# Attention scores by groups of four heads in TensorE's rows, and moved earlier in a two-layer hybrid encoder

## The chip, the cores and the metric

The kernel runs on one core of a Trainium2 chip. The metric is the device time of one execution in microseconds (us), the median of several executions.

## The reference

An encoder of two layers over 256 tokens with 1024 channels, in float32. Each layer mixes tokens in three parallel branches (multi-head latent attention, a convolution module, bidirectional retention), merges them by gates, and applies a SwiGLU block. The change concerns the attention branch alone:

```python
def mla_branch(c_q, c_kv, k_pe, cos, sin, q_norm, w_uq, kv_norm, w_ukv, w_o):
    q = (rms_norm(c_q, q_norm) @ w_uq).reshape(B, S, MLA_HEADS, MLA_NOPE + MLA_ROPE)   # 8 heads, 64 + 32
    q_nope = q[..., :MLA_NOPE]
    q_pe = apply_rope(q[..., MLA_NOPE:], cos, sin)
    kv = (rms_norm(c_kv, kv_norm) @ w_ukv).reshape(B, S, MLA_HEADS, MLA_NOPE + MLA_V)  # 8 heads, 64 + 64
    k_nope, v = kv[..., :MLA_NOPE], kv[..., MLA_NOPE:]
    k_pe = apply_rope(k_pe, cos, sin)                                                  # one key for all heads
    scale = (MLA_NOPE + MLA_ROPE) ** -0.5
    ...
        s = (jnp.einsum('bqhd,bkhd->bhqk', qn, k_nope)
             + jnp.einsum('bqhr,bkr->bhqk', qp, k_pe))
        p = jax.nn.softmax(s.astype(jnp.float32) * scale, axis=-1).astype(v.dtype)
        return jnp.einsum('bhqk,bkhd->bqhd', p, v)
    ...
    return o @ w_o
```

A head's score is the sum of a plain part over 64 channels and a rotary part over 32 channels, whose key all heads share.

## The kernel before

Activations lie transposed (channels on the 128 partitions, the 256 tokens along the row) as two halves in fp32r, `hT`; every weight is loaded in units of 128x1024, of which ScalarE makes the high half (`whi`, a cast, L175) and VectorE the low half (`wlo`, a subtraction, L177). Each product is three fp32r matmuls (L186, L187, L188). There are 9 buffers for high halves and 8 for low halves, so a unit is made some 8 units before TensorE reads it.

A layer runs, in TensorE's order: the latent projections, four groups for the convolution module, the up-projections of the attention (`up_T`, L577), then four groups for the retention's queries and keys (RQ, RQ, RK, RK: `feat_group`, 48 matmuls of 256 columns each, in two halves of 24), then three groups of its values and gates (RV, RG, RG: `tok_group`, four units of 12 matmuls of 512 columns each), then the gate groups and everything behind.

Small work of other branches is put between these matmuls. The list `pe_steps` holds closures; `feat_group` takes one from it after each of its halves, `tok_group` one after each of its units. So the place of a step in the list decides after which half or unit TensorE meets it. The steps of attention are:

- `qpe_T` (L602): transposes of the rotated query parts, copied to `qT`.
- `mla_b(pr)` (L626): the scores of a pair of heads, four fp32 matmuls over 96 rows, into two PSUM banks from the pool `tp` of four; then VectorE's row maximum `nm` (L629), ScalarE's exponentials into `pe` with sums `sme` (L634), VectorE's reciprocal (L636) and ScalarE's scaling of `pe` (L639).
- `mla_c(pr)` (L651): eight transposes of `pe`, copied by ScalarE to `pT` (L652).
- `mla_d(pr)` (L662): the products with the values `vtok`, two heads side by side in 64 columns each, split to `oTr`.

The four pairs' b, c and d steps (12) fill the 12 places of the RV, RG and RG groups: b(0) after RV's first unit, b(1) after the second, c(0) after the third, and so on to d(3) after the last unit of the second RG group.

VectorE also does the convolution: 124 operations per layer on `cacc` (L531, L534; "taps" below), which wait in a list of their own, `vec_steps`, two of which are issued with each weight unit. A list scheduler orders the instructions of every engine when the program is built, by its own estimate of when each can start; at run time each engine works through its own list in that order.

The score rows of a head lie in one buffer, plain part on partitions 0 to 63 and rotary part on 64 to 95, which is why each up-projection bank (two heads above each other on 128 partitions) is copied out in two activations of 64 partitions (L577), and the rotary parts in four of 32 (L605).

Of the kernel before, what the change touches and what calls it, by code (L numbers as in the profile page):

```python
# [58 lines left out]
def tile_hybrid_encoder(  # L59
# [63 lines left out]
    warm = act.tile([P, 512], BF16, tag="half", name="warm", bufs=7)  # L123
# [205 lines left out]
    kpad = cst.tile([P, NB, QK], F32, tag="kpad", name="kpad")  # L329
    G.memset(kpad, 0.0)  # L330

    def setup_tables():
# [3 lines left out]
        pos_r = act.tile([P, 512], I32, tag="half", name="pos_r", bufs=7)[:, :SEQ]  # L336
# [72 lines left out]
    for l in range(DEPTH):  # L409
# [23 lines left out]
        kT = big("kT").rearrange("p (h n) -> p h n", h=MH)  # L433
# [19 lines left out]
        def latent(pa, b):  # L453
# [11 lines left out]
            tk = sm.tile([P, ROPE], F32, tag="tk", name="tk", bufs=2)  # L465
            rope(kpad[:, b, NOPE:].rearrange(V4, h=1, j=2),
                 pa[:, QR + KVR:C_CONV].rearrange(V4, h=1, j=2),
                 cosr[:, b, :], sinr[:, b, :], tk.rearrange(V4, h=1, j=2))

            def f():  # L470
                pc = tp()
                for j in range(3):
                    T.transpose(pc[:, j * P:(j + 1) * P], cn[:, j * P:(j + 1) * P], ident)
                T.transpose(pc[:QK, 3 * P:4 * P], kpad[:, b, :], ident)
# [68 lines left out]
        qT = big("qT").rearrange("p (h n) -> p h n", h=MH)  # L543
# [45 lines left out]
        for c in range(2):  # L589
            up_T(qT[:, 4 * c:4 * c + 4, :], un[c], 0, (cTh, cTl), 0, 2, sc)()  # L590
        for c in range(2):
            up_T(kT[:, 4 * c:4 * c + 4, :], uk, c, (cTh, cTl), 2, 1, 1.0)()
# [5 lines left out]
        def qpe_T():  # L598
# [10 lines left out]
        for g in range(2):  # L609
            feat_group(win, C_RQ + g * 256, hT, KT, ret_rope(rqT, g))  # L610
        for g in range(2):
            feat_group(win, C_RK + g * 256, hT, KT, ret_rope(rkT, g))
# [5 lines left out]
        NPR = MH // 2  # L618
        pTs, pes = {}, {}

        def mla_b(pr):
            def f():
                for b in range(NB):
                    ps = tp()
                    for j in range(2):
                        T.matmul(ps[:, j * SEQ:(j + 1) * SEQ], qT[:QK, 2 * pr + j, b * P:(b + 1) * P],  # L626
                                 kT[:QK, 2 * pr + j, :], start=True, stop=True)
# [4 lines left out]
                    for j in range(2):  # L632
                        js = slice(j * SEQ, (j + 1) * SEQ)
                        S.activation(pe[:, js], ps[:, js], AF.Exp, bias=nm[:, j:j + 1],  # L634
                                     accum_out=sme[:, j:j + 1])
                    V.reciprocal(sme, sme)  # L636
                    for j in range(2):
                        js = slice(j * SEQ, (j + 1) * SEQ)
                        S.activation(pe[:, js], pe[:, js], AF.Copy, scale=sme[:, j:j + 1])  # L639
                    pes[pr, b] = pe  # L640
            return f

        def mla_c(pr):
            def f():
                pT = mid("pT").rearrange("p (h k n) -> p h k n", h=2, k=2)
                pTs[pr] = pT
                for b in range(NB):
                    pe = pes.pop((pr, b))
                    pt = tp()
                    for jk in range(4):  # L650
                        T.transpose(pt[:, jk * P:(jk + 1) * P], pe[:, jk * P:(jk + 1) * P], ident)  # L651
                    S.copy(pT[:, :, :, b * P:(b + 1) * P],  # L652
                           pt.rearrange("p (h k n) -> p h k n", h=2, k=2))
# [29 lines left out]
        def ret_a(h):  # L683
            def f():
# [17 lines left out]
                sh = act.tile([P, 512], F32R, tag="half", name="sTh", bufs=7)  # L702
                sl = act.tile([P, 512], F32R, tag="half", name="sTl", bufs=7)
# [284 lines left out]
```

## Time and profile before

| | |
|---|---|
| median of 3 runs | 934.07 us (933.36 to 934.19) |
| profiled execution: its own time | 933.89 us |
| profiled execution: span of the trace | 932.1 us |
| granted TensorE clock, mean | 0.998 |
| TensorE matmul busy | 924.0 us (99% of the span) |
| VectorE busy | 689.0 us (74%) |
| ScalarE busy | 530.9 us (57%) |

Busy time of TensorE counts from a matmul's start to its modelled end, and neighbours overlap; what a matmul costs is read from the distance of its start to the next one's. Times in the trace count from the start of the span, which is 1.8 us shorter than the execution's own time.

### The profile page before, as it was taken

The page shows a single profiled execution, that of the slowest core. Times are in us where ns is not written, and L with a number is a line of the kernel's source. Part 1 is how long each engine was busy: PE and PEld are TensorE (multiplying, and loading weights), DVE is VectorE, ACT ScalarE, POOL GpSimd, SP SyncE. Part 2 cuts the span into 40 slices and gives each one's busy share as a digit, 9 for nine tenths or more (in the row PEclk, how much of TensorE's full clock was granted, in tenths as well). Part 3 has the DMA queues.
Part 4 walks back from the last instruction along what each step waited for, and adds up shares of the span by engine and source line. Part 5 has one row for each costly group of instructions (what it writes and reads, how often), then busy time and mean ns, then how long its engine had stood idle before and what let it go on. Part 6 is the DMA issues. An engine that isn't in the chain of part 4 may idle for free.

```text
span 932.1 us, 13255 instructions
## 1 busy us (share of the span) xinstructions
PE 924.0 (99%) x4924; PEld 788.9 (85%) x4924; DVE 689.0 (74%) x1101; ACT 530.9 (57%) x821; POOL 36.7 (4%) x77
## 2 busy tenths in 40 slices
PE   9999999999999999999999999999999999999997
PEld 6999878888888888888889997788888888888885
DVE  6789999996657766664485899999766676666532
ACT  5774786545545655554365758755454556566421
POOL 2000000000010000000120000010000100000000
PEclk9999999999999999999999999999999999999999
DMA  6885455565637766666377655545656376665621
GB/s 226 250 270 161 137 173 164 158 185 185 191 88 234 248 183 191 191 203 193 100 210 204 183 157 174 188 136 162 200 181 177 123 236 191 194 186 182 214 79 45
DMA packets 113214, 166.70 MB, mean 179 GB/s; under 512 B 5929, under 2 KB 62905, under 8 KB 113150
## 3 DMA queue, kind: packets, MB, share of 16 engines
q1 hardware_dynamic: 113150, 165.87, 58.5%
q8 instruction: 38, 0.62, 0.3%
q14 instruction: 26, 0.21, 0.1%
HBM read 164.80 MB, written 1.05 MB: 178 GB/s over the span
## 4 chain that ended last, share of the span: by engine, by line
PE 97%; DMA 1%; ACT 0%; DVE 0%; SPq 0%; issue 0%; DVEq 0%; POOLq 0%; POOL 0%; ACTq 0%
PE acc L186 20%; PE acc L187 19%; PE acc L188 19%; PE acc L251 12%; PE acc L253 7%; PE acc L205 6%; PE acc L208 3%; PE acc L254 2%; PE tp L626 1%; PE tp L662 1%; PE tp L651 1%; DMA raw<-in_w_in_dram 1%; PE tp L692 1%; PE tp L283 1%; PE tp L187 1%; PE tp L188 1%
## 5 line engine op out<-in xcount | busy, mean ns | idle before, releaser
L177 DVE TENSOR_TENSOR wlo<-raw,whi 128x1024 fp32r<-128x1024 f32 (+1 forms) x300 | 362.7, 1216 | 119.7 <-PE acc L187 58.4
L175 ACT CAST whi<-raw 128x1024 fp32r<-128x1024 f32 (+1 forms) x300 | 312.2, 1048 | 200.9 <-PE acc L188 120.5
L251 PE MATMUL acc<-hT,whi 128*128 128x512 f32 x504 | 127.8, 393 | 0.0
L186 PE MATMUL acc<-whi,hT 128*128 128x512 f32 x288 | 118.2, 410 | 0.0
L187 PE MATMUL acc<-wlo,hT 128*128 128x512 f32 x288 | 112.7, 391 | 0.0
L188 PE MATMUL acc<-whi,hT 128*128 128x512 f32 x288 | 112.6, 391 | 0.0
L251 PEld LDWEIGHTS acc<-hT,whi 128*128 128x128 f32 x504 | 94.7, 189 | 18.3
L534 DVE SCALAR_TENSOR_TENSOR cacc<-apad,ccol,cacc 128x256 f32<-128x256 f32 x240 | 108.4, 479 | 1.3
L253 PEld LDWEIGHTS acc<-hT,wlo 128*128 128x128 f32 x576 | 78.6, 190 | 5.6
L253 PE MATMUL acc<-hT,wlo 128*128 128x256 f32 x576 | 80.3, 282 | 0.0
L186 PE MATMUL acc<-hT,whi 128*128 128x256 f32 x256 | 73.2, 286 | 0.0
L188 PE MATMUL acc<-hT,wlo 128*128 128x256 f32 x256 | 72.5, 283 | 0.0
L187 PE MATMUL acc<-hT,whi 128*128 128x256 f32 x256 | 72.5, 283 | 0.0
L186 PE MATMUL acc<-whi,hidh 128*128 128x512 f32 x176 | 68.6, 390 | 0.0
L188 PE MATMUL acc<-whi,hidl 128*128 128x512 f32 x176 | 68.5, 389 | 0.0
L187 PE MATMUL acc<-wlo,hidh 128*128 128x512 f32 x176 | 68.5, 389 | 0.0
L186 PEld LDWEIGHTS acc<-whi,hT 128*128 128x128 f32 x288 | 54.2, 188 | 13.3 <-issue 3.1
L188 PEld LDWEIGHTS acc<-whi,hT 128*128 128x128 f32 x288 | 54.1, 188 | 12.1
L187 PEld LDWEIGHTS acc<-wlo,hT 128*128 128x128 f32 x288 | 54.3, 189 | 10.1
L205 PE MATMUL acc<-whi,hT 128*128 128x512 f32 (+1 forms) x128 | 49.6, 389 | 0.4 <-ACT hT L182 0.3
L186 PEld LDWEIGHTS acc<-hT,whi 128*128 128x128 f32 x256 | 49.1, 192 | 0.2
L187 PEld LDWEIGHTS acc<-hT,whi 128*128 128x128 f32 x256 | 49.1, 192 | 0.2
(248 smaller groups left out, 1478.3 us busy)
## 6 DMA issues: line engine op xcount, KB each, us to landing
raw<-in_w_in_dram SPq DMA_DIRECT2D x112, 512.0 KB, 4.0
raw<-in_ffn_w_gate_dram SPq DMA_DIRECT2D x44, 512.0 KB, 4.3
raw<-in_ffn_w_up_dram SPq DMA_DIRECT2D x44, 512.0 KB, 4.6
raw<-in_ffn_w_down_dram SPq DMA_DIRECT2D x44, 512.0 KB, 4.4
raw<-in_ret_w_o_dram SPq DMA_DIRECT2D x16, 512.0 KB, 3.7
raw<-in_w_out_dram SPq DMA_DIRECT2D x16, 512.0 KB, 3.7
raw<-in_mla_w_o_dram SPq DMA_DIRECT2D x8, 512.0 KB, 4.4
raw<-in_conv_w_pw_dram SPq DMA_DIRECT2D x8, 512.0 KB, 3.7
```

Of the source, the lines that this page charges most:

```text
L175: S.copy(hi, raw)
L177: V.tensor_sub(lo, raw, hi.bitcast(F32))
L186: T.matmul(o, lh, rh, start=start, stop=False)
L187: T.matmul(o, lh, rl, start=False, stop=False)
L188: T.matmul(o, ll, rh, start=False, stop=stop)
L205: T.matmul(o, ah[:, 2 * i + k, :], w[:, k, :], start=not (i or k or n), stop=False)
L208: T.matmul(o, al[:, 2 * i - 2 + k, :], units[i - 1][0][:, k, :], start=False, stop=i == len(units) and k == 1)
L251: T.matmul(ps, units[k // 4][0][:, k % 4, js], both[:, k, :], start=k == 0, stop=False)
L253: T.matmul(ps[:, SEQ:], units[k // 4][1][:, k % 4, js], both[:, k, :SEQ], start=False, stop=False)
L254: T.matmul(ps, units[-1][0][:, 3, js], both[:, KT - 1, :], start=False, stop=True)
L283: T.transpose(ps[:, j * P:(j + 1) * P], hn[:, (4 * c + j) * P:(4 * c + j + 1) * P], ident)
L534: V.scalar_tensor_tensor(cacc[:, j, :], src, ccol[:, j, w:w + 1], cacc[:, j, :], op0=ALU.mult, op1=ALU.add)
```

## The change

The plain parts of two heads now lie above each other on the 128 partitions (`qn`, `kn`: four such pairs), and the rotary parts of four heads likewise (`qp`; the shared key `kp` is repeated four times). So an up-projection bank leaves in one activation of 128 partitions, and so do the rotary parts. A score is now the sum of two matmuls in a PSUM bank: one over 64 rows (two heads occupy the two halves of TensorE's rows) and one over 32 rows (four heads, four quarters). One `mla_b` step does four heads: 8 matmuls over 64 rows and 8 over 32, into all four `tp` banks, one for each head. There are two such steps instead of four, and c and d stay per pair. The steps start earlier: right after `qpe_T` in the RQ groups, not in RV.

```diff
-        return act.tile([P, 1024], F32, tag="mid", name=name, bufs=5)
+        return act.tile([P, 1024], F32, tag="mid", name=name, bufs=7)
...
-        return act.tile([P, 512], F32, tag="half", name=name, bufs=7)
+        return act.tile([P, 512], F32, tag="half", name=name, bufs=9)
...
-    kpad = cst.tile([P, NB, QK], F32, tag="kpad", name="kpad")
-    G.memset(kpad, 0.0)
+    kpad = cst.tile([P, NB, 4, ROPE], F32, tag="kpad", name="kpad")
...
-                S.copy(kT[NOPE:QK, :, b * P:(b + 1) * P],
-                       pc[NOPE:QK, 3 * P:4 * P].unsqueeze(1).broadcast_to([ROPE, MH, P]))
+                T.transpose(pc[:, 3 * P:4 * P], kpad[:, b].rearrange("p r n -> p (r n)"), ident)
+                S.copy(kp[:, b * P:(b + 1) * P], pc[:, 3 * P:4 * P])
...
-                pv = pq.rearrange("p (j n) -> p j n", j=2)
-                for i in range(2):
-                    S.activation(dst[:NOPE, i::2, :], pv[i * NOPE:(i + 1) * NOPE], AF.Copy, scale=scale)
+                S.activation(dst, pq.rearrange("p (j n) -> p j n", j=2), AF.Copy, scale=scale)
...
-            pv = pt.rearrange("p (g n) -> p g n", g=2)
-            for i in range(4):
-                S.copy(qT[NOPE:QK, i::4, :], pv[i * ROPE:(i + 1) * ROPE])
-        pe_steps.append(qpe_T)
+            S.copy(qp, pt.rearrange("p (g n) -> p g n", g=2))
...
-        def mla_b(pr):
+        def mla_b(qd):
+            def f():
+                banks = [tp() for _ in range(4)]
+                def out(r, b):
+                    return banks[r][:, b * SEQ:(b + 1) * SEQ]
+                for p in range(2):
+                    for b in range(NB):
+                        for i in range(2):
+                            hs = slice(i * NOPE, (i + 1) * NOPE)
+                            T.matmul(out(2 * p + i, b), qn[hs, 2 * qd + p, b * P:(b + 1) * P],
+                                     kn[hs, 2 * qd + p, :], start=b == 0, stop=False)
                 for b in range(NB):
-                    ps = tp()
-                    for j in range(2):
-                        T.matmul(ps[:, j * SEQ:(j + 1) * SEQ], qT[:QK, 2 * pr + j, b * P:(b + 1) * P],
-                                 kT[:QK, 2 * pr + j, :], start=True, stop=True)
+                    for r in range(4):
+                        rs = slice(r * ROPE, (r + 1) * ROPE)
+                        T.matmul(out(r, b), qp[rs, qd, b * P:(b + 1) * P], kp[rs, :], start=False, stop=b == 1)
+                for r in range(4):
+                    ps = banks[r]
...
-        for t in range(NPR + 2):
-            for d, stage in ((0, mla_b), (1, mla_c), (2, mla_d)):
-                if 0 <= t - d < NPR:
-                    pe_steps.append(stage(t - d))
+        pe_steps.extend([qpe_T, nop, mla_b(0), nop, nop, mla_c(0), mla_c(1), mla_d(0),
+                         mla_d(1), mla_b(1), nop, nop, mla_c(2), mla_c(3), mla_d(2), mla_d(3)])
+        for g in range(2):
+            feat_group(win, C_RQ + g * 256, hT, KT, ret_rope(rqT, g))
+        for g in range(2):
+            feat_group(win, C_RK + g * 256, hT, KT, ret_rope(rkT, g))
```

The small operations per bank (maximum, exponentials, reciprocal, scaling) are as many as before and of the same shapes; the four heads of a step come behind each other. The shared rotary key is made in as many VectorE operations as before.

Where the first scores stand in VectorE's list, before: the end of the second RK rotation (L446 to L450 is one rotation of a group's output), and then the maxima `nm` of the first pair, each with one tap (L534) between.

```order
L446 TENSOR_TENSOR rkT<-acc,cosT 128x512
L448 TENSOR_TENSOR rt<-acc,sinT 64x512
L449 TENSOR_TENSOR rt<-acc,sinT 64x512
L534 SCALAR_TENSOR_TENSOR cacc<-apad,ccol,cacc 128x256
L450 TENSOR_TENSOR rkT<-rkT,rt 128x512
L534 SCALAR_TENSOR_TENSOR cacc<-apad,ccol,cacc 128x256
L629 TENSOR_REDUCE nm<-tp 128x2
L534 SCALAR_TENSOR_TENSOR cacc<-apad,ccol,cacc 128x256
L629 TENSOR_REDUCE nm<-tp 128x2
```

The same place in the changed kernel, from the end of the first RQ rotation on (taps are L538, maxima L635, reciprocals L641 there):

```order
L449 TENSOR_TENSOR rt<-acc,sinT 64x512
L538 SCALAR_TENSOR_TENSOR cacc<-apad,ccol,cacc 128x256
L450 TENSOR_TENSOR rqT<-rqT,rt 128x512
L538 SCALAR_TENSOR_TENSOR cacc<-apad,ccol,cacc 128x256
L177 TENSOR_TENSOR wlo<-raw,whi 128x1024
L538 SCALAR_TENSOR_TENSOR cacc<-apad,ccol,cacc 128x256 x11
L635 TENSOR_REDUCE nm<-tp 128x2 x4
L538 SCALAR_TENSOR_TENSOR cacc<-apad,ccol,cacc 128x256
L177 TENSOR_TENSOR wlo<-raw,whi 128x1024
L641 RECIPROCAL sme<-sme 128x2 x2
L446 TENSOR_TENSOR rqT<-acc,cosT 128x512
```

Eleven taps stand ahead of the four maxima, and the rotation of the second RQ group, which stood five rows behind the first one's end, now stands behind the maxima and two reciprocals.

Where the second four heads' scores stand in VectorE's list of the changed kernel (before, the corresponding third pair's two maxima stood behind one `wlo` and the two halves of `vrl`):

```order
L177 TENSOR_TENSOR wlo<-raw,whi 128x1024
L538 SCALAR_TENSOR_TENSOR cacc<-apad,ccol,cacc 128x256 x8
L535 TENSOR_SCALAR cacc<-apad,ccol 128x256
L538 SCALAR_TENSOR_TENSOR cacc<-apad,ccol,cacc 128x256
L635 TENSOR_REDUCE nm<-tp 128x2 x3
L641 RECIPROCAL sme<-sme 128x2
L635 TENSOR_REDUCE nm<-tp 128x2
L641 RECIPROCAL sme<-sme 128x2
```

Ten taps stand ahead of these maxima. Between the two places VectorE's list of the changed kernel holds the rotations of the last three groups, six `wlo` units, the low halves of the first two `oTr` parts and single taps.

ScalarE's list for the second four heads in the changed kernel (exponentials are L640, scalings L644, `pT` copies L659):

```order
L640 ACTIVATE pe,sme<-tp,nm 128x256 x4
L644 ACTIVATE pe<-pe,sme 128x256 x4
L640 ACTIVATE pe,sme<-tp,nm 128x256 x4
L644 ACTIVATE pe<-pe,sme 128x256 x4
L182 CAST vrh<-acc 128x512 x2
L175 CAST whi<-raw 128x1024 x2
L659 COPY pT<-tp 128x512 x2
```

The scaling of the first of the four heads stands behind the exponentials of the first two; the copies of the first `pT` stand behind all four heads, two `vrh` and two weight casts.

## Rows read from the trace of the kernel before

**Rows 1.** The page: busy time of the engines, share of the span, instructions.

```profile
PE 924.0 (99%) x4924; PEld 788.9 (85%) x4924; DVE 689.0 (74%) x1101; ACT 530.9 (57%) x821; POOL 36.7 (4%) x77
```

**Rows 2.** Stretches: length, busy us (instructions) of PE, PEld, DVE, ACT, POOL, clock.

```profile
71.80:112.10 40.30, 40.30 (x255) 36.40 (x253) 40.06 (x71) 24.91 (x53) 0.00 (x0) 1.00 0.54 156
528.70:569.00 40.30, 40.30 (x254) 36.45 (x253) 40.06 (x71) 26.20 (x54) 0.00 (x0) 1.00 0.54 156
```

**Rows 3.** Timeline of TensorE: start, duration, line, rows*columns of the array, shape, count.

```profile
68.65 0.28 PE L187 MATMUL acc<-hT,whi 128*128 128x256 f32 x1
...
88.68 0.40 PE L186 MATMUL acc<-whi,hT 128*128 128x512 f32 x1
...
91.43 1.89 PE L626 MATMUL tp<-kT,qT 96*128 96x256 f32 x8
...
93.40 0.40 PE L187 MATMUL acc<-wlo,hT 128*128 128x512 f32 x1
```

**Rows 4.** Timeline of TensorE at mla_d(0), two heads in 64 columns each.

```profile
112.38 1.08 PE L662 MATMUL tp<-pT,vtok 128*64 128x256 f32 x8
...
113.73 0.40 PE L187 MATMUL acc<-wlo,hT 128*128 128x512 f32 x1
```

**Rows 5.** Timeline of TensorE where it goes to 34 and then 8 rows.

```profile
36.23 0.28 PE L188 MATMUL acc<-hT,wlo 128*128 128x256 f32 x1
36.44 0.43 PE L503 MATMUL tp<-ident,prow 34*128 34x34 f32 x4
36.80 0.23 PE L504 MATMUL tp<-ident,grow 8*128 8x8 f32 x1
```

**Rows 6.** Timeline of VectorE in layer 0: one rotation, and a run of the other operations.

```profile
72.78 0.69 DVE L446 TENSOR_TENSOR rqT<-acc,cosT 128x512 f32<-128x512 f32 x1
...
74.90 0.49 DVE L534 SCALAR_TENSOR_TENSOR cacc<-apad,ccol,cacc 128x256 f32<-128x256 f32 x1
75.31 0.69 DVE L450 TENSOR_TENSOR rqT<-rqT,rt 128x512 f32<-128x512 f32 x1
75.91 0.48 DVE L534 SCALAR_TENSOR_TENSOR cacc<-apad,ccol,cacc 128x256 f32<-128x256 f32 x1
...
103.69 2.05 DVE L534 SCALAR_TENSOR_TENSOR cacc<-apad,ccol,cacc 128x256 f32<-128x256 f32 x5
105.66 1.22 DVE L177 TENSOR_TENSOR wlo<-raw,whi 128x1024 fp32r<-128x1024 f32 x1
106.79 1.28 DVE L183 TENSOR_TENSOR vrl<-acc,vrh 128x512 fp32r<-128x512 f32 x2
107.99 1.28 DVE L629 TENSOR_REDUCE nm<-tp 128x2 f32<-128x512 f32 x2
109.19 0.87 DVE L534 SCALAR_TENSOR_TENSOR cacc<-apad,ccol,cacc 128x256 f32<-128x256 f32 x2
109.97 0.16 DVE L636 RECIPROCAL sme<-sme 128x2 f32<-128x2 f32 x1
110.05 0.86 DVE L534 SCALAR_TENSOR_TENSOR cacc<-apad,ccol,cacc 128x256 f32<-128x256 f32 x2
```

**Rows 7.** Timeline of TensorE at mla_c(0) and mla_c(1).

```profile
100.38 1.25 PE L651 MATMUL tp<-ident,pe 128*128 128x128 f32 x8
...
108.68 1.03 PE L651 MATMUL tp<-ident,pe 128*128 128x128 f32 x8
...
109.78 0.40 PE L187 MATMUL acc<-wlo,hT 128*128 128x512 f32 x1
```

**Rows 8.** Timeline of ScalarE behind the third pair's maxima.

```profile
108.72 0.50 ACT L634 ACTIVATE pe<-tp,nm 128x256 f32<-128x256 f32 x1
...
110.53 1.74 ACT L639 ACTIVATE pe<-pe,sme 128x256 f32<-128x256 f32 x4
112.13 2.02 ACT L175 CAST whi<-raw 128x1024 fp32r<-128x1024 f32 x2
114.02 1.10 ACT L652 COPY pT<-tp 128x512 f32<-128x512 f32 x2
```

More of the change, by code (lines that the diff above doesn't have):

```diff
@@ L122, in tile_hybrid_encoder @@
     V.memset(ones, 1.0)
-    warm = act.tile([P, 512], BF16, tag="half", name="warm", bufs=7)
+    warm = act.tile([P, 512], BF16, tag="half", name="warm", bufs=9)
     G.memset(warm, 0.0)
@@ L335, in setup_tables @@
                           allow_slow_non_contiguous=True)
-        pos_r = act.tile([P, 512], I32, tag="half", name="pos_r", bufs=7)[:, :SEQ]
+        pos_r = act.tile([P, 512], I32, tag="half", name="pos_r", bufs=9)[:, :SEQ]
         nc.sync.dma_start(pos_r, positions[0].partition_broadcast(P))
@@ L432, in tile_hybrid_encoder @@
         cTh, cTl = (cT[:, i * 768:(i + 1) * 768].rearrange("p (k n) -> p k n", k=3) for i in range(2))
-        kT = big("kT").rearrange("p (h n) -> p h n", h=MH)
+        kT = big("kT")
+        kn, kp = kT[:, :1024].rearrange("p (h n) -> p h n", h=MH // 2), kT[:, 1024:1024 + SEQ]
         vrh, vrl = (big(n, F32R).rearrange("p (b n) -> p b n", b=NB) for n in ("vrh", "vrl"))
@@ L464, in latent @@
                                    op0=ALU.mult, op1=ALU.mult)
[L465 to L468, printed above, removed]
+            tk = sm.tile([P, 2, 2, HR], F32, tag="tk", name="tk", bufs=2)
+            kr = pa[:, QR + KVR:C_CONV].rearrange("p (j n) -> p j n", j=2)
+            V.tensor_tensor(tk[:, 0], kr, cosr[:, b, :].unsqueeze(1).broadcast_to([P, 2, HR]), op=ALU.mult)
+            V.tensor_tensor(tk[:, 1, 0, :], kr[:, 1, :], sinr[:, b, :], op=ALU.mult)
+            V.tensor_tensor(tk[:, 1, 1, :], kr[:, 0, :], sinr[:, b, :], op=ALU.mult)
+            for j, op in enumerate((ALU.subtract, ALU.add)):
+                V.tensor_tensor(kpad[:, b, :, j * HR:(j + 1) * HR],
+                                tk[:, 0, j, :].unsqueeze(1).broadcast_to([P, 4, HR]),
+                                tk[:, 1, j, :].unsqueeze(1).broadcast_to([P, 4, HR]), op=op)
             def f():
@@ L540, in tile_hybrid_encoder @@
         drain(pe_steps)
-        qT = big("qT").rearrange("p (h n) -> p h n", h=MH)
+        qT = big("qT")
+        qn, qp = (qT[:, i:i + n * SEQ].rearrange("p (h n) -> p h n", h=n) for i, n in ((0, MH // 2), (1024, 2)))
         vtok = mid("vtok").rearrange("p (b h d) -> p b h d", b=NB, h=MH)
@@ L589, in tile_hybrid_encoder @@
         for c in range(2):
[L590 removed]
+            up_T(qn[:, 2 * c:2 * c + 2, :], un[c], 0, (cTh, cTl), 0, 2, sc)()
         for c in range(2):
[L592 removed]
+            up_T(kn[:, 2 * c:2 * c + 2, :], uk, c, (cTh, cTl), 2, 1, 1.0)()
         for b in range(NB):
@@ L631, in f @@
                     sme = sm.tile([P, 2], F32, tag="sme", name="sme")
[L632 to L635, printed above, removed]
+                    for b in range(NB):
+                        bs = slice(b * SEQ, (b + 1) * SEQ)
+                        S.activation(pe[:, bs], ps[:, bs], AF.Exp, bias=nm[:, b:b + 1], accum_out=sme[:, b:b + 1])
                     V.reciprocal(sme, sme)
[L637 to L640, printed above, removed]
+                    for b in range(NB):
+                        bs = slice(b * SEQ, (b + 1) * SEQ)
+                        S.activation(pe[:, bs], pe[:, bs], AF.Copy, scale=sme[:, b:b + 1])
+                    pes[4 * qd + r] = pe
             return f
@@ L646, in f @@
                 pTs[pr] = pT
-                for b in range(NB):
-                    pe = pes.pop((pr, b))
+                for j in range(2):
+                    pe = pes.pop(2 * pr + j)
                     pt = tp()
[L650 to L653, printed above, removed]
+                    for k in range(NB):
+                        for b in range(NB):
+                            T.transpose(pt[:, k * SEQ + b * P:k * SEQ + (b + 1) * P],
+                                        pe[:, b * SEQ + k * P:b * SEQ + (k + 1) * P], ident)
+                    S.copy(pT[:, j], pt.rearrange("p (k n) -> p k n", k=2))
             return f
@@ L701, in f @@
                                            op0=ALU.mult, op1=ALU.mult)
-                sh = act.tile([P, 512], F32R, tag="half", name="sTh", bufs=7)
-                sl = act.tile([P, 512], F32R, tag="half", name="sTl", bufs=7)
+                sh = act.tile([P, 512], F32R, tag="half", name="sTh", bufs=9)
+                sl = act.tile([P, 512], F32R, tag="half", name="sTl", bufs=9)
                 split(sh, sl, sT)
```

8 lines of the change are left out of this document (1 added, 7 removed).

## The prediction

> **What bounds the kernel now.** I read the page first: matmuls are busy 99% of the span [rows 1]. So the time is the sum of what TensorE works through, plus its waits. I then read the timeline of TensorE, start to start. A 512-column matmul takes 0.23 us (12 of them from 88.68 to 91.43), a 256-column one 0.12 us (167 from 68.65 to 88.68) [rows 3]. A pair's scores, four fp32 matmuls recorded as eight, push the next products back by 93.40 - 91.43 - 0.23 = 1.74 us, 0.435 us for one, and nothing more is lost at their edges [rows 3]. Any matmul time saved here comes straight off the total, unless TensorE has to wait instead.
>
> So the second reading is of who could make it wait. In the stretch where the attention steps will now lie, VectorE is busy 40.06 of 40.30 us, in both layers alike [rows 2]. It works through a fixed list without gaps, mostly taps that nobody needs soon, and it is not late for TensorE: only one c step waits, the first, whose eight records last 1.25 us where another's last 1.03, so 0.22 us [rows 7]. Idle time of VectorE could absorb a badly placed tap; there is none. This decides the case.
>
> **TensorE's own work.** Four heads cost 2 x 1.74 = 3.48 us before. Now there are eight matmuls over 64 rows and eight over 32. No row shows two matmuls in different rows at once. The nearest is mla_d, two heads in different columns: eight 256-column records take only about four slots, with 113.73 - 112.38 - 0.23 = 1.12 us behind their start [rows 4]. I take rows to overlap as columns do: four slots for the plain pairs, two for the rotary fours, six of 0.435 us, 2.61 us together. Edges: going from 128 rows to 34 costs 0.21 us in place of 0.12, so 0.09 [rows 5]; with that, mla_d costs 1.21 us, of which two slots are 0.87 and going in and out 0.34. The step to 32 rows between plain and rotary parts lies between 0.09 (the 34 to 8 rows' start, after four short transposes) and some 0.2 with a weight load laid bare; I take 0.2 [rows 4, 5]. A block is then 2.61 + 0.34 + 0.20 = 3.15 us. The gain is 0.33 us for four heads, **0.66 us per layer**. Ends: without any overlap the block is 16 x 0.435 + 0.54 = 7.5 us; with the pairs alone 12 x 0.435 + 0.54 = 5.8.
>
> The 0.22 us wait of the first c step goes too. The c and d steps stay at 109.78 - 108.68 - 0.23 = 0.87 us [rows 7] and 1.21. The fewer ScalarE copies (up-projections, rotary parts, shared key) save engine time that TensorE was not waiting for; I cost them at nothing. They are covered on both sides: an earlier copy meets the same matmul stream. The wider key operations are small, and the larger pools take no time.
>
> **What is late next.** TensorE ends the first RQ group at 88.68 - 144 x 0.12 = 71.4 us, as before. By the new order it meets, after RQ's second group's first half, the first score block, three halves later c(0), and so on. VectorE begins the first rotation when that bank is there: at the earliest 71.4, before at 72.78 [rows 6]; with ScalarE's copies out of the way I take 71.8. Durations, start to start [rows 6]: a rotation 2.12 + 0.60 = 2.72; a tap 1.97/5 = 0.394; a `wlo` 1.13; a maximum 0.60; a reciprocal 0.08; an `oTr` low half, 256 columns as a tap has, 0.394.
>
> - First four heads. Ahead of the first maximum stand a rotation, 13 taps and one `wlo`: 2.72 + 5.12 + 1.13, so it ends at 71.8 + 8.97 + 0.6 = 81.4. The scores are done by 77.5 (71.4 + 2.88 + 3.15), so they wait 3 us for VectorE. Exponentials at 0.45 us each and scalings at 0.40 [rows 8] end for head 1 at about 86.4, after the reciprocals, which stand behind another tap and `wlo`. TensorE comes to c(0) at 71.4 + 4 x 2.88 + 3.15 = 86.1, and needs head 1 at 86.5. Just in time: no wait, at most 1 us.
> - Second four heads. Up to the fifth maximum the list holds 4 rotations, 9 `wlo`, 41 taps or tap-like, 5 maxima and 4 reciprocals: 10.88 + 10.17 + 16.15 + 3.0 + 0.32 = 40.5 us, so it ends at 112.3. Four exponentials (1.8) and four scalings (1.6) follow on ScalarE: head 4 is ready at 115.0, head 5 at 115.8. TensorE arrives at c(2) at 88.68 + 5 units x 2.75 + 2 blocks x 3.15 + 2 x 0.87 + 2 x 1.21 = 112.9. Its eight transposes end at 116.3 in place of 113.8: **2.5 us of waiting**. All matmuls of the second RG group and everything behind stand behind this.
> - The next c(3) is met at 119.0 with its heads ready at 118.4 and 119.2: none. d(2) needs the copies of `pT`, which ScalarE has behind the other heads' 3.4 us, two `vrh` (0.95), two casts (1.89) and themselves (1.0) [rows 8], a `vrh` taken as a `pT` copy: 123.0. TensorE is there at 122.7: **0.4 us**. d(3) is met in time.
> - Weight units: casts stop while the exponentials run, but units are made eight ahead; by the same list each `wlo` of this stretch is done over 10 us before it is read. No wait. By the same durations the retention's first `sT` comes some 5 us later than before, half a microsecond before it is read; no wait taken, up to 1 us possible.
>
> Sum per layer: -0.66 - 0.22 + 2.5 + 0.4 = +2.0 us, both layers +4.0. On the profiled execution's 933.89 that is 937.9; the median of the runs lies 0.18 higher, so **938.0 us**, +0.4%. The sum hangs little on the price of a block. A longer block shortens the wait by as much, since VectorE's list, not TensorE, says when c(2) can go; a block may cost 4.2 us before the total moves. By the same token VectorE's list may be off by 1% (0.4 us) and its start by 0.4 lower or 1.0 higher, twice: 936.2 to 940.5 for this case.
>
> The Trainium skill (TensorEngine Tiling (Array Packing), PSUM Bottleneck) warns that tiling speeds up TensorE but not the evacuation of PSUM, which may then become the bottleneck. Here the evacuation is those maxima and exponentials, as many as before. By the rule the gain of 0.66 us is the part that cannot be had, and the sum has it so.
>
> **Rivals.**
> - *The wait does not come*: the maxima run near when the scores are done, and only the matmul gain is left: -0.88 per layer, 932.3 us. For it: before, one c step alone waited, and 0.22 us [rows 7]. Against: eleven and ten taps now stand ahead of the maxima, at full load. It decides when c(2)'s heads are ready 2.5 us earlier, which is six taps out of the way. With half of the wait, 935.
> - *Pairs overlap, fours don't*: block 5.8 us. TensorE then comes to c(2) at 118.1, later than its heads; no wait. 2 x (5.8 - 3.48) - 0.22 = +4.4 per layer, 942.8 us. For it: four weight loads and four PSUM banks at once appear in no row.
> - *No overlap*: block 7.5, +8.0 - 0.2 per layer, 949.6 us. Against: the column pairs of mla_d do overlap, in fp32 [rows 4].
> - *More waits*: c(0) and the retention's first step each lose up to 1 us per layer as well: 940 to 943.
>
> The Trainium skill (TensorE: Matmul & The Clock Gate, Part 3: Packing small matmuls) has four row tiles of 32 rows and 512 columns run 3.07 times as fast as one after the other. No row here shows that; by it the two rotary slots are 0.26 us longer in all and the block 3.4 us, with the same sum, since the wait takes it up.
>
> **How the numbers follow.** My forecast (wait of about 2 to 3 us at c(2) in each layer) 0.57; the wait small or gone 0.22, of which 0.13 within 0.2% of before and 0.09 below; fours not overlapping 0.08; no overlap 0.06; more waits 0.07. A measurement of this kernel tells about 0.2% (1.9 us) from no change. So slower 0.78, within 0.13, faster 0.09 (932.2 or less). The range leaves out the no-overlap case and some 0.13 of the small-wait case: 933.5 to 943.0.
>
> **What would show it.** Right: a block of six slots with its records starting in pairs and fours a few ns apart, some 3.1 us long; TensorE idle ahead of L657 at c(2) by 2 to 3 us, ended by ScalarE's L644, in both layers 457 us apart; the maxima L635 ending some 7 us after their scores; VectorE without a gap from 72 to 112. Wrong: records of a block one behind the other (a later rival); L635 directly behind the scores (the first); a wait ended by a weight (`whi`, `wlo`), of which I expect none. What would make it wrong above all is VectorE reaching the second maxima earlier than 112.

## The result, and the profile after

The changed kernel takes 938.88 us (median of 6 runs, 937.66 to 941.67), beside it the kernel before 933.86 (933.23 to 934.34): ratio 1.0052, 95% interval [1.0041, 1.0062], slower. Its profiled execution took 938.17 us, with a span of 936.4. The prediction was 938.0.

The page of the changed kernel: the engines' line, and the first line of the chain of work that ended last.

```profile
PE 923.7 (99%) x4988; PEld 787.1 (84%) x4988; DVE 688.0 (73%) x1101; ACT 510.0 (54%) x803; POOL 37.7 (4%) x76
...
PE 90%; DVE 7%; DMA 1%; issue 1%; ACT 0%; SPq 0%; DVEq 0%; POOLq 0%; POOL 0%; ACTq 0%
```

By the first line hardly anything happened [rows 1]. The second tells more: the chain before was PE 97% and DVE 0%; now it runs through VectorE for 7% of the span, some 33 us in each layer. The stretches of [rows 2], after:

```profile
71.80:112.10 40.30, 38.73 (x287) 32.94 (x286) 39.94 (x76) 18.67 (x39) 0.00 (x0) 1.00 0.44 131
528.70:569.00 40.30, 38.73 (x295) 33.30 (x294) 39.94 (x73) 21.02 (x41) 0.00 (x0) 1.00 0.44 132
```

VectorE is as full as before; TensorE, which had no gap here, now has 1.57 us of idle time in each layer, at full clock. Where that is, the timeline of TensorE shows, around the first and the second block of scores [rows 3]:

```profile
74.67 0.28 PE L188 MATMUL acc<-hT,wlo 128*128 128x256 f32 x1
74.88 2.00 PE L626 MATMUL tp<-kT,qT 64*128 64x256 f32 x16
76.81 1.15 PE L631 MATMUL tp<-kT,qT 32*128 32x256 f32 x16
77.89 0.38 PE L186 MATMUL acc<-hT,whi 128*128 128x256 f32 x1
78.11 0.28 PE L187 MATMUL acc<-hT,whi 128*128 128x256 f32 x1
...
101.82 0.39 PE L188 MATMUL acc<-whi,hT 128*128 128x512 f32 x1
102.14 1.56 PE L626 MATMUL tp<-kT,qT 64*128 64x256 f32 x10
105.27 1.13 PE L626 MATMUL tp<-kT,qT 64*128 64x256 f32 x6 [1.57 <-DVE oTr L183]
106.33 1.15 PE L631 MATMUL tp<-kT,qT 32*128 32x256 f32 x16
107.40 0.50 PE L186 MATMUL acc<-whi,hT 128*128 128x512 f32 x1
```

The first block is as predicted: 77.89 - 74.67 - 0.12 = 3.10 us and another 0.10 of exposed weight load behind it (78.11 - 77.89 - 0.12), 3.2 in all (3.15 predicted). The second stops in its middle, after ten of its records, until VectorE has written the low half of `oTr` (L183). That is the output of mla_d(1), which lies in the fourth `tp` bank; the block needs all four. From the tenth record's start to the eleventh's it takes 1.94 us, where 0.22 is usual; and the two heads that the stop tears apart no longer run as a pair, which costs the block another 0.5 us. VectorE's own timeline [rows 6] shows why that is late, and what follows:

```profile
103.66 1.22 DVE L177 TENSOR_TENSOR wlo<-raw,whi 128x1024 fp32r<-128x1024 f32 x1
104.79 0.42 DVE L183 TENSOR_TENSOR oTr<-tp,oTr 128x256 fp32r<-128x256 f32 x1
105.13 0.48 DVE L538 SCALAR_TENSOR_TENSOR cacc<-apad,ccol,cacc 128x256 f32<-128x256 f32 x1
...
108.19 3.25 DVE L538 SCALAR_TENSOR_TENSOR cacc<-apad,ccol,cacc 128x256 f32<-128x256 f32 x8
111.36 0.41 DVE L535 TENSOR_SCALAR cacc<-apad,ccol 128x256 f32<-128x256 f32 x1
111.68 0.48 DVE L538 SCALAR_TENSOR_TENSOR cacc<-apad,ccol,cacc 128x256 f32<-128x256 f32 x1
112.08 1.88 DVE L635 TENSOR_REDUCE nm<-tp 128x2 f32<-128x512 f32 x3
```

ScalarE has done the high half of this output at 102.9; the low half stands in VectorE's full list like everything else and is written 1.9 us later. The scores are done at 107.4; the ten taps ahead of their maxima hold these up to 112.08. ScalarE's timeline behind them [rows 8], and TensorE's at c(2) and d(2) [rows 4, 7]:

```profile
112.80 0.47 ACT L640 ACTIVATE pe<-tp,nm 128x256 f32<-128x256 f32 x1 [8.81 <-DVE nm L635]
...
114.61 1.71 ACT L644 ACTIVATE pe<-pe,sme 128x256 f32<-128x256 f32 x4
...
120.54 2.04 ACT L175 CAST whi<-raw 128x1024 fp32r<-128x1024 f32 x2
122.44 1.10 ACT L659 COPY pT<-tp 128x512 f32<-128x512 f32 x2
```

```profile
115.51 0.39 PE L188 MATMUL acc<-whi,hT 128*128 128x512 f32 x1
115.74 1.18 PE L657 MATMUL tp<-ident,pe 128*128 128x128 f32 x8
116.67 0.48 PE L186 MATMUL acc<-whi,hT 128*128 128x512 f32 x1
...
123.23 1.45 PE L668 MATMUL tp<-pT,vtok 128*64 128x256 f32 x8
124.61 0.50 PE L186 MATMUL acc<-whi,hT 128*128 128x512 f32 x1
```

At c(2), where 2.5 us of waiting were forecast, TensorE waits some 0.1 us: it comes there at 115.7, 2.8 us later than forecast (the stop in the block, and 0.5 of a later start, below), just when the heads are ready. At d(2) it loses 0.36.

The 4.28 us between the two profiled executions: 0.51 in the start (the transposes L507 begin at 36.95, L503 before at 36.44), 1.82 and 1.81 from there to the first retention step in the two layers, 0.12 and 0.10 in the retention, -0.08 elsewhere. The start I take to be no work of the change: the start of these transposes moves between 35.9 and 38.9 us over the kernels below, whose programs are nearly alike up to there. The granted clock from 6 to 18 us is 0.70 and 0.73 in this execution and 1.00 in that of before, but that alone does not set it: taps later, below, has 1.00 there too and starts them at 38.3. So the stretch **from the column transposes to the first retention step** is what I compare from here on: 103.58 us before (36.44 to 140.01), 105.40 after (36.95 to 142.35).

### The profile page after: what moved, and what is told of

It reads as the page before. It is cut to its first block, busy times and chain, and to the rows that moved or that the text cites. A ratio compares the mean times of both kernels' runs of the same rounds, so it can differ in the third digit from the quotient of the medians.

```text
span 936.4 us, 13315 instructions
## 1 busy us (share of the span) xinstructions
PE 923.7 (99%) x4988; PEld 787.1 (84%) x4988; DVE 688.0 (73%) x1101; ACT 510.0 (54%) x803; POOL 37.7 (4%) x76
## 4 chain that ended last, share of the span: by engine, by line
PE 90%; DVE 7%; DMA 1%; issue 1%; ACT 0%; SPq 0%; DVEq 0%; POOLq 0%; POOL 0%; ACTq 0%
PE acc L186 18%; PE acc L188 18%; PE acc L187 18%; PE acc L251 12%; PE acc L253 7%; PE acc L205 6%; PE acc L208 3%; DVE cacc L538 2%; PE acc L254 2%; DVE wlo L177 1%; PE tp L702 1%; DMA raw<-in_w_in_dram 1%; DVE rt L448 1%; DVE rt L449 1%; PE tp L283 1%
## 5 line engine op out<-in xcount | busy, mean ns | idle before, releaser
L251 PEld LDWEIGHTS acc<-hT,whi 128*128 128x128 f32 x504 | 94.6, 188 | 18.4
L538 DVE SCALAR_TENSOR_TENSOR cacc<-apad,ccol,cacc 128x256 f32<-128x256 f32 x240 | 105.7, 482 | 0.6
L186 PEld LDWEIGHTS acc<-hT,whi 128*128 128x128 f32 x256 | 49.0, 191 | 0.9 <-issue 0.7
L205 PE MATMUL acc<-wlo,hT 128*128 128x512 f32 (+1 forms) x128 | 49.5, 387 | 0.0
```

The costliest lines, as they stand in the source:

```text
L186: T.matmul(o, lh, rh, start=start, stop=False)
L205: T.matmul(o, ah[:, 2 * i + k, :], w[:, k, :], start=not (i or k or n), stop=False)
L251: T.matmul(ps, units[k // 4][0][:, k % 4, js], both[:, k, :], start=k == 0, stop=False)
L538: V.scalar_tensor_tensor(cacc[:, j, :], src, ccol[:, j, w:w + 1], cacc[:, j, :], op0=ALU.mult, op1=ALU.add)
```

## Experiments

All times are medians, and each ratio is against runs of the kernel before on the same chip beside it: 933.86 us for the kernel as changed, 934.87, 934.85 and 935.88 for the next twelve, four by four in the order of the table. So the ratios compare between rows, and the times only within such a group; a ratio can differ by some units of its fourth place from the quotient of these medians. "Taps" counts those on VectorE between the start of the first RQ rotation and the first `sTl` of the retention, layer 0.

| kernel | us | ratio [95%] | stretch, layer 0 | taps |
|---|---|---|---|---|
| before | | 1 | 103.58 | 69 |
| as changed | 938.88 | 1.0052 [1.0041, 1.0062] | 105.40 | 87 |
| step before b(1) | 940.52 | 1.0063 [1.0051, 1.0075] | 105.44 | 87 |
| step behind b(1) | 939.84 | 1.0054 [1.0039, 1.0068] | 106.42 | 87 |
| bank emptied by ScalarE | 940.76 | 1.0063 [1.0051, 1.0076] | 106.70 | 88 |
| bank and step | 938.67 | 1.0051 [1.0038, 1.0064] | 104.63 | 88 |
| taps later | 938.62 | 1.0036 [1.0022, 1.0051] | 102.61 | 41 |
| taps later, pairs | 958.67 | 1.0236 [1.0216, 1.0255] | 103.37 | 21 |
| taps later and step | 944.37 | 1.0092 [1.0078, 1.0107] | 102.61 | 38 |
| rows apart | 938.94 | 1.0035 [1.0024, 1.0046] | 105.26 | 87 |
| early pairs | 934.16 | 0.9980 [0.9969, 0.9990] | 103.13 | 69 |
| late fours | 944.18 | 1.0089 [1.0077, 1.0102] | 108.88 | 89 |
| rotary twice | 954.16 | 1.0193 [1.0178, 1.0208] | 113.76 | 105 |
| taps from RV on | 933.39 | 0.9972 [0.9962, 0.9983] | 102.61 | 67 |

### The bank, or the list

My theory after the trace: VectorE's list sets when TensorE may go on, and b(1), c(2), d(2) are only the places where that is felt. The rival: only the late fourth bank costs.

**One empty step ahead of b(1).**

```diff
-                         mla_d(1), mla_b(1), nop, nop, mla_c(2), mla_c(3), mla_d(2), mla_d(3)])
+                         mla_d(1), nop, mla_b(1), nop, nop, mla_c(2), mla_c(3), mla_d(2), mla_d(3)])
```

> One empty step is put between mla_d(1) and mla_b(1), so the bank of d(1) has 2.75 us more to be freed before the second block needs it. Both theories: the 1.94 us gap inside the second block goes. List theory (VectorE's list decides): with the step the list gets one wlo (1.13) and four taps (4 x 0.394) more ahead of the fifth maximum, which ends 2.7 us later (115 instead of 112.3); TensorE comes to c(2) at 115.7, its heads are ready near 118, so about 2.4 us of waiting stand at c(2) instead; d(2)'s 0.6 us stay. Time as changed, 938.9 us (938.0 to 939.5). Bank theory (only the late bank costs, the heads of c(2) are ready in time): 2 x 1.74 less, and the 0.3 at c(2) as well: 934.8 us.

The block no longer waits, and TensorE's timeline at c(2) is this:

```profile
116.93 0.39 PE L188 MATMUL acc<-whi,hT 128*128 128x512 f32 x1
118.90 1.74 PE L657 MATMUL tp<-ident,pe 128*128 128x128 f32 x8 [1.58 <-ACT pe L644]
```

118.90 - 116.93 - 0.23 = 1.74 us and 0.7 more within the eight transposes (two starts 0.40 us apart, where 0.11 is usual): 2.4 us at c(2), as the list theory said, and the stretch is the same, 105.44. In layer 1 a lower clock (0.50 from 580 to 582 us) follows this wait, and the stretch takes 106.64.

**One empty step behind b(1)**, the same edit one place later:

```diff
-                         mla_d(1), mla_b(1), nop, nop, mla_c(2), mla_c(3), mla_d(2), mla_d(3)])
+                         mla_d(1), mla_b(1), nop, nop, nop, mla_c(2), mla_c(3), mla_d(2), mla_d(3)])
```

> One empty step more between mla_b(1) and mla_c(2); the place of the second block and VectorE's list ahead of the fifth maximum are unchanged. List and bank theory alike: the 1.74 us lost in the second block stay, the 0.3 us at c(2) and the 0.6 us at d(2) go, since TensorE comes 2.75 us later to both: 2 x 0.9 less, 937.1 us (936.5 to 938.0). If the distance between b(1) and c(2) alone were what counts (my prediction's reading, the loss at c(2)), the whole loss would go: 934.0 us.

The waits at c(2) and d(2) went and that in the block stayed (1.95 us from start to start), as expected; the time did not fall, though. Behind the wait the granted clock fell: 0.50, its lower level of 1.2 GHz, from 106 to 108 us, and 0.84 and 0.81 in the two us on either side. That cost the stretch the gain and another microsecond. It came in both layers here, in neither layer of the kernel as changed, whose block waits as long.

**The bank emptied by ScalarE** instead of by the split:

```diff
-                split(oTh[:, pr, :], oTl[:, pr, :], po[:, :SEQ])
+                of = half("of")[:, :SEQ]
+                S.copy(of, po[:, :SEQ])
+                split(oTh[:, pr, :], oTl[:, pr, :], of)
```

> The output of each mla_d is first copied out of its bank by ScalarE, and split from there, so the bank no longer waits for VectorE's low half; VectorE's list ahead of the fifth maximum is as long as before (112.3). List theory: the gap inside the second block goes, TensorE comes to c(2) about 1.7 us earlier, at 113, and waits there for its heads until 115.3: 2.0 to 2.5 us, as first predicted; time unchanged, 938.9 us (938.2 to 939.5; four more ScalarE copies of 0.3 us each layer can add some tenths at d(2)). Bank theory: 2 x 1.74 less, 935.4 us.

TensorE's timeline at c(2), and the stretches from 116 us on (columns as in [rows 2]):

```profile
112.79 0.39 PE L188 MATMUL acc<-whi,hT 128*128 128x512 f32 x1
114.77 1.96 PE L657 MATMUL tp<-ident,pe 128*128 128x128 f32 x8 [1.60 <-ACT pe L644]
```

```profile
116.00:118.00 2.00, 2.00 (x7) 1.71 (x8) 2.00 (x6) 2.00 (x10) 0.00 (x0) 0.54 0.06 7
118.00:120.00 2.00, 2.00 (x7) 1.53 (x6) 2.00 (x7) 2.00 (x6) 0.00 (x0) 0.61 0.80 255
```

This is the prediction's own scene: with the bank out of the way TensorE finishes its last product ahead of c(2) at 113.0 (112.9 forecast) and waits there 1.75 us and again 0.7 within, 2.4 together (2.5 forecast). Again a lower clock follows the wait and adds about 1.3 us to the stretch. The bank theory, with 935.4, is out.

**Both edits.**

> Both edits: ScalarE empties the bank of mla_d, and one empty step more stands between mla_b(1) and mla_c(2). List theory: the second block has its banks, TensorE comes to c(2) at 115.7, where the heads are ready at about 115.3, and to d(2) after the copies: no wait is left, 2 x (1.74 + 0.3 + 0.6) = 5.3 less than changed, 933.6 us, and 0.5 less where the clock is full from the start (932.5 to 934.0). If it is not the waits but the block of scores or the early place itself that costs (say a lower clock behind it), the time stays above 937.

No wait is left at c(2), nor in the block of layer 0 (0.5 us in that of layer 1), and the clock stays up. The stretch is 0.8 us shorter than as changed, and still nothing is won in the total: what lies behind it, the retention first, takes 1.0 us (layer 0) and 1.4 us (layer 1) more than in the kernel as changed. Some of what TensorE's weight loads wait for from 110 to 152 us (us in total, times, longest):

```profile
PEld tp L668 <- ACT pT L659: 2.1, 2, 1.8
PEld tp L186 <- ACT sTh L182: 1.0, 1, 1.0
PEld tp L188 <- DVE sTl L183: 0.4, 1, 0.4
```

These are the next things in line: the `pT` copies for d(2) (1.9 us of the stretch), behind casts on ScalarE, and the retention's first `sT`, which VectorE now makes at 147.4 us where before it was at 141.2. A step's place does not help when the list itself is longer.

### The taps

The list of the kernel as changed holds 87 taps ahead of the retention's first `sTl`, that of before 69. Eighteen taps are 7.1 us of VectorE, and the first `sTl` begins 77.0 us after the first rotation instead of 69.9.

**Taps later**: none is given to the scheduler while RQ to RG run, then six with each unit. The unit's `drain(vec_steps, TAPS)` becomes `drain(vec_steps, taps[0])`, and

```diff
+        taps[0] = 0
         qT = big("qT")
...
+        taps[0] = 6
         onT = []
```

> Kernel as changed, but the convolution's taps are given to the scheduler only behind the RG groups, so that none stands in VectorE's list ahead of the maxima: by the same durations the list reaches the fifth maximum as soon as its scores are there (its sum is 97 us instead of 112.3) and the first sTl at 130 instead of 149.6. All taps are still done, later. List theory: no wait in the second block, at c(2) or in the retention, d(2) at most 0.6 us; a layer from its column transposes to its retention takes 103.6 - 0.66 - 0.22 = 102.7 us instead of 105.4, so 938.9 - 5.4 = 933.5 us (932.3 to 934.5), if the later taps make nothing else late. If banks, ScalarE or the clock held TensorE up, the time stays above 937.

The stretch is 102.61 us, 102.7 expected, and none of the waits above is left in it: this shows VectorE's list as the cause. But 3.4 us come back later in layer 0, where the remaining taps run in one piece ahead of weight units (from 195 to 240 us):

```profile
PEld acc L188 <- DVE wlo L178: 2.8, 2, 2.0
```

**The kernel before with the same edit**, and **taps later with a step more**:

> The kernel before with the same later taps, as the control of the run above. Its one wait, 0.22 us at the first c step, may go, nothing else is to be had: 933.4 us (933.0 to 934.5). What the run above stays below this one is what the four heads' block gives by itself: 2 x 0.66 = 1.3 us by my price of a block (3.15 against 3.48).

> Later taps and one empty step more between mla_b(1) and mla_c(2), for the wait at d(2), which is ScalarE's (exponentials, scalings and copies in one queue). List theory: the same as with later taps alone or up to 0.6 us a layer less: 932.3 to 933.5 us, the fastest of all kernels here. If c and d become late for the retention instead, as with the bank and the step, 935 or more.

Both ran into the same trouble, and worse: 21 and 38 taps are done ahead of the first `sTl`, so 103 and 86 of the 124 fall behind it, and TensorE waits for `wlo` units and for `cacc` there. As controls of the total they fail; in the stretch itself the pairs take 103.37, so that the change has 0.76 us less without waits.

### The order that the scheduler makes

Why are there more taps ahead at all? Two theories: the early place of the steps, or the sixteen matmuls in place of eight in a block, which the scheduler takes for longer than they are.

**Early pairs**: the kernel before, its old score layout, at the change's places (`two` makes one step of two pairs).

```diff
-        pe_steps.append(qpe_T)
-        for g in range(2):
-            feat_group(win, C_RQ + g * 256, hT, KT, ret_rope(rqT, g))
...
+        pe_steps.extend([qpe_T, nop, two(mla_b(0), mla_b(1)), nop, nop, mla_c(0), mla_c(1), mla_d(0),
+                         mla_d(1), two(mla_b(2), mla_b(3)), nop, nop, mla_c(2), mla_c(3), mla_d(2), mla_d(3)])
+        for g in range(2):
+            feat_group(win, C_RQ + g * 256, hT, KT, ret_rope(rqT, g))
```

> The kernel before with its steps where the change has them (two pairs in one step each, ahead of RQ and RK), but its old score layout: 8 matmuls over 128 rows for four heads instead of 16 over 64 and 32. Its VectorE list has 20 taps ahead of the fifth maximum (39 as changed) and 69 ahead of the first sTl (87 as changed, 69 before). Order theory (the scheduler puts matmuls one behind the other in its plan, so 16 in place of 8 make it fill VectorE with 18 more taps, 7.1 us, that TensorE then waits for): no wait of more than some tenths, 933.5 us (932.8 to 934.5). Place theory (the early place makes TensorE meet a full VectorE): 937 or more.

No wait for data of the other engines above 0.4 us, and faster than before by 0.2%. The taps alone (columns: stretch, its length, busy time of PE, PEld, DVE, then clock and DMA) between the first rotation and the first `sTl`, in the kernel as changed, in this one and in rotary twice, below:

```profile
72.20:149.12 76.92, 0.00 (x0) 0.00 (x0) 36.86 (x87) 1.00 0.49 152
```

```profile
74.30:143.96 69.66, 0.00 (x0) 0.00 (x0) 29.80 (x69) 1.00 0.53 168
```

```profile
72.30:156.86 84.56, 0.00 (x0) 0.00 (x0) 44.01 (x105) 0.96 0.44 139
```

Early or late, pairs have 69: the early place does not bring the taps.

**Late fours**: the change's blocks five places later.

```diff
-        pe_steps.extend([qpe_T, nop, mla_b(0), nop, nop, mla_c(0), mla_c(1), mla_d(0),
+        pe_steps.extend([qpe_T, nop, nop, nop, nop, nop, nop, mla_b(0), nop, nop, mla_c(0), mla_c(1), mla_d(0),
```

> The change's score layout with its steps five drains later, about where the kernel before has them. Its list has 56 taps ahead of the fifth maximum and 89 ahead of the first sTl, which by the durations of the prediction ends at 150.3 (142.5 before). Order theory: TensorE waits some tenths to 1.5 us at c(0), the second block, c(2) and the retention, pinned by that sTl: 939 us (937.5 to 941). Place theory (late is right): the block's gain alone, 932.5 us.

89 taps, slower than before, so the place theory fails here too: c(0), c(1) and c(2) lose 1.9 us in each layer. But it lies 8.3 us above the kernel before, where I had 5. TensorE's timeline at d(3), and ScalarE's:

```profile
135.82 1.08 PE L668 MATMUL tp<-pT,vtok 128*64 128x256 f32 x8
139.35 2.46 PE L668 MATMUL tp<-pT,vtok 128*64 128x256 f32 x8 [2.45 <-ACT pT L659]
```

```profile
135.68 1.28 ACT L697 ACT_TABLE_LOAD   x1
...
137.79 1.03 ACT L175 CAST whi<-raw 128x1024 fp32r<-128x1024 f32 x1
138.73 1.06 ACT L659 COPY pT<-tp 128x512 f32<-128x512 f32 x2
```

The last `pT` copy has got behind the retention's decay tables on ScalarE; I had summed VectorE's list alone. And I had overlooked that the list now holds 21 steps for 20 places, so that d(3) stands directly behind d(2), with no weight unit (2.75 us) between: the copies end at 139.8, about when d(3) would have been met with a unit between (4.0 us behind d(2), as in the kernel before). So this wait, 2.6 us here and 2.7 in layer 1, is in good part the edit's own and says nothing on the order. A clock of 0.50 from 140 to 142 us follows in layer 0.

**Rotary twice**: eight more matmuls of 32 rows in each block, so that the rotary part counts double and the output is no longer the encoder's.

```diff
-                for b in range(NB):
+                for b, n in ((0, 0), (0, 1), (1, 0), (1, 1)):
```

> Kernel as changed, but each rotary matmul is done twice into the same sum (the rotary part of the scores counts double): eight more matmuls of 32 rows in a block, which in fours take 2 x 0.435 = 0.87 us, 3.5 us in four blocks. Price theory (TensorE's own time goes to the total): 942.4 us. Cover theory (as predicted: a block may cost 4.2 us before the total moves): 938.9. Order theory: the scheduler fills VectorE for sixteen more matmuls a layer one behind the other: 57 taps ahead of the fifth maximum and 105 ahead of the first sTl, 18 more than as changed, 7.1 us, for which TensorE waits at c(2) or later: 2 x 7 more, 952 us (948 to 954).

105 taps (the last fence above), another 18 for another sixteen matmuls, and 954.16 us beside 935.88 of the kernel before: 18.3 us more, where the order theory had 952 - 933.9 = 18.1, the price theory 8.5 and the cover theory 5. That it fits so closely is in part chance: in the traced execution three stretches at lower clock, which no theory had, are in it. The matmuls themselves are cheap, 0.86 us for a block. TensorE waits at c(2), 122.33 - 119.17 - 0.23 = 2.9 us there alone, and 1.9 at c(0):

```profile
119.17 0.39 PE L188 MATMUL acc<-whi,hT 128*128 128x512 f32 x1
122.33 1.74 PE L657 MATMUL tp<-ident,pe 128*128 128x128 f32 x8 [2.77 <-ACT pe L644]
```

So sixteen matmuls more on separate rows bring eighteen taps, 16 x 0.435 = 7.0 us against 18 x 0.394 = 7.1: just what a plan would do that sets them one behind the other, and fills VectorE for so long. The scheduler's plan itself was not read; that it works so is inferred from these counts.

**Rows apart** was meant to price the overlap, by putting matmuls of the same rows behind each other (the loops over `b` and over `i`, or `r`, exchanged).

```diff
-                    for b in range(NB):
-                        for i in range(2):
+                    for i in range(2):
+                        for b in range(NB):
...
-                for b in range(NB):
-                    for r in range(4):
+                for r in range(4):
+                    for b in range(NB):
```

> Kernel as changed, with the matmuls of a block in another order: the two for the same rows follow each other, so only neighbours of different rows can overlap. Five slots for eight plain matmuls and five for eight rotary ones instead of four and two: a block of 10 x 0.435 + 0.54 = 4.9 us instead of 3.15, 7 us more in four blocks. List theory (TensorE's own time hardly counts while it waits for VectorE): the waits in the second block, at c(2) and at d(2) go, the fifth maximum stands at 110.7 in the list, a layer takes 103.6 - 0.22 + 2 x 1.42 = 106.2 instead of 105.4: 940.5 us (939.5 to 941.5). If the price of a block goes straight to the total: 945.9 us.

It tells nothing on that: the scheduler put pairs and fours together again, and the first block takes 3.3 us (3.2 as changed). Only VectorE's list differs by some taps: the fifth maximum comes earlier, the gap in the second block shrinks from 1.94 to 0.59 us, and d(2) loses 0.6 us more than as changed. The stretch stays at 105.26. Once more a wait moved and the sum stayed.

### A version that is faster than both

**Taps from RV on**: the hold on the taps ends ahead of RV, with two for each unit as before.

```diff
+        taps[0] = 0
         qT = big("qT")
...
+        taps[0] = 2
         gs = big("gs").rearrange("p (b n) -> p b n", b=NB)
```

> Kernel as changed, the taps held back only while RQ and RK run and given to the scheduler from RV on: 18 taps ahead of the fifth maximum (104 us by the list), 67 ahead of the first sTl and 79 ahead of the fourth, as before the change (69 and 81). List and order theory: no wait in the attention, a layer's stretch 102.6 us as with all taps later, and nothing late for the convolution: 933.9 - 2 x 0.97 = 931.9 us (931.0 to 933.5, by the start), faster than both kernels. If holding taps back makes the convolution late again, 935 to 938.

Faster than the kernel before by 0.28% [0.17, 0.38]. Both stretches take 102.6 us, no wait for data is left in them, and nothing comes back later: the rest of each layer takes what it took before (to 0.2 us). The first four heads in this kernel, and in the one with early pairs, on TensorE:

```profile
76.63 0.28 PE L189 MATMUL acc<-hT,wlo 128*128 128x256 f32 x1
76.84 2.00 PE L628 MATMUL tp<-kT,qT 64*128 64x256 f32 x16
78.76 1.15 PE L633 MATMUL tp<-kT,qT 32*128 32x256 f32 x16
79.84 0.38 PE L187 MATMUL acc<-hT,whi 128*128 128x256 f32 x1
```

```profile
75.56 0.28 PE L188 MATMUL acc<-hT,wlo 128*128 128x256 f32 x1
75.68 3.62 PE L617 MATMUL tp<-kT,qT 96*128 96x256 f32 x16
78.95 0.47 PE L186 MATMUL acc<-hT,whi 128*128 128x256 f32 x1
```

79.84 - 76.63 - 0.12 = 3.09 and 0.10 behind it, against 78.95 - 75.56 - 0.12 = 3.27 and 0.19: the change is worth 0.27 us for four heads, and twice that, 0.53, is the difference of the two stretches (103.13 and 102.60).

## Why the prediction was right, and where not

- **What decides**: right. "VectorE's list decides when c(2) can go." Without the taps in it the loss is gone; with it no place of the steps helps. VectorE began its first rotation at 72.1 (71.8 taken), the first maximum at 81.14 (80.8), the fifth at 112.08 (111.7): sums of a list with one duration for each kind of operation hold to half a microsecond over 40.
- **The step that failed**: "2.5 us of waiting" at c(2). It did not come there: TensorE lost 0.14 us at these transposes (L657), so the sign that the prediction named for itself, 2 to 3 us idle there, failed. I summed what c(2) waits for and looked at no wait of the second block itself, though it takes all four `tp` banks and mla_d(1)'s output lies in one. That bank is freed by a row of the same full list, so the block waited first. Against the version with no waits the block lost 2.26 us, c(2) 0.14 and d(2) 0.36: 2.8, where I had 2.5 + 0.4. The sum came out right because the list sets the end of c(2), whichever wait comes first; the bank emptied by ScalarE shows the wait at the place predicted, with 2.4 us.
- **"The sum hangs little on the price of a block"**: wrong as a rule. In a given order it may hold, since waits take up what is saved (rows apart was meant to show it and did not); but the order is made anew for each kernel, and by the runs each matmul more brings a good tap more ahead of what TensorE waits for. 0.87 us more per block, 3.5 in all, cost some 13 us (a ratio of 1.0193 in place of 1.0052, low-clock stretches included), not nothing. By the same token I gave no reason for the "eleven and ten taps" that stand ahead of the maxima: I took the list as it was and put its load down to no cause, which early pairs and late fours show to be the score matmuls' number.
- **TensorE's own gain**: 0.66 us a layer predicted, 0.53 measured; the block costs 3.19 (3.15 forecast) and four heads in pairs 3.46 (3.48), so the gain is 0.27 a block, not 0.33. Pairs moved together and early saved 0.45 (0.22 predicted for the first c step alone).
- **Sum**: per layer -0.53 - 0.45 + 2.8 = +1.82 in the trace, +2.0 predicted. That the profiled execution's 938.2 lies so near the 937.9 forecast for it is in part luck: the layers have 0.4 us less than forecast, the start 0.5 and the retention 0.2 more. By its own terms (0.4 and 0.4 lower, 0.4 and 1.0 higher, twice) the range given for this case would be 936.4 to 940.8, not 936.2 to 940.5.
- **Rivals**: fours do overlap. Their sixteen records take 77.89 - 76.81 = 1.08 us, where one behind the other they would take 8 x 0.435 = 3.48, 3.2 times as long. The Trainium skill (TensorE: Matmul & The Clock Gate, Part 3: Packing small matmuls) has 3.07 for four row tiles of 32 rows and 512 columns; the trace, with 256 columns in fp32, agrees. "More waits" did not come: c(0) costs what it costs in taps from RV on, and behind the stretch only 0.12 and 0.10 us are lost. "The wait does not come" is what taps from RV on makes of the kernel: 0.28% below before, 932.3 predicted for it, 0.2%.
- **Evacuation**: the Trainium skill (TensorEngine Tiling (Array Packing), PSUM Bottleneck) says that tiling speeds up TensorE but not the emptying of PSUM, which may become the bottleneck. The runs agree only in part. The 0.53 us could be had in full as soon as other work stood behind the maxima; it was not the evacuation's amount that ate it, but its place in the queue.

## What to carry to other kernels

When a scheduler orders the queues, a change on one engine can reorder the others, here, as the counts suggest, by what the scheduler believes that it costs; so compare the whole list of the engine that is full, counting what stands ahead of each thing that is waited for, and not only the lines that the change touches. A wait that was pinned by a full queue did not go away here with the place of a step: it came back at the next thing in line, a bank, a copy, an `sT`; give the urgent work its place ahead of the filler. And for a step that takes every buffer of a pool, ask first who frees the last one.

## What the runs showed of the hardware

- Matmuls on separate rows run at the same time, in fp32 too: records of a block start in pairs and in fours 6 to 14 ns apart, the next pair or four 216 ns later, weight loads as well. A change of the rows used costs some 0.2 us at each place (64 to 32 rows, 32 to 128), in gaps and an exposed weight load: from 64 to 32 rows the next start comes 305 ns after the last, and the one behind it 320, where 216 is usual.
- After an idle time of 1.7 to 2.9 us in a stream at full clock, the granted clock was 0.50 (1.2 GHz) for some 3 to 4 us in several executions (behind the second block in both layers of one kernel, behind c(2) in both layers of another and in one of two of a third; in rotary twice behind c(0) in both layers and behind c(2) in one, in late fours at one of the two d(3)), and not after the like idle time in both layers of the kernel as changed, nor after 2.6 us at the other d(3). Where it could be told apart, such a stretch cost 1.2 to 1.5 us. What decides whether it comes is open.
- The start of the program differs by up to 3 us from one execution to the next (35.9 to 38.9 us to the same transposes), in kernels that are nearly alike up to there; what sets it is open.
